# First modulation, second half's norm and its modulation on VectorE alone, GpSimd without arithmetic until the convolution

## Chip, cores and metric

The kernel runs on one core of a Trainium2 chip. The metric is the device time of one execution in microseconds (us). Five engines of the core are named by their roles: TensorE multiplies matrices, VectorE and GpSimd do arithmetic between tiles, ScalarE does activations, scalings and casts, and SyncE (SP) issues the DMA transfers. In the rows of the profile they are PE, DVE, POOL, ACT and SP.

## What is computed

The reference is a stack of two layers on a latent stream x of 1024 tokens by 1024 channels, all in float32. Layer 0 is a convolution module, layer 1 a pooling mixer; each is one modulated sub-layer with a residual:

```python
sh, sc, gt = split(silu(c) @ w_mod[i] + b_mod[i], 3)      # three vectors of 1024
h = rms(x, norm_g[i]) * (1.0 + sc) + sh
x = x + gt * mixer_i(h)

def conv_mixer(h):                                         # layer 0
    a, b, g = split(h @ w_in, 3)
    y = depthwise_conv(a * sigmoid(b), dw, 31 taps) + db
    return (silu(layernorm(y)) * silu(g)) @ w_out

def pool_mixer(h):                                         # layer 1
    v, g = split(h @ w_in, 2)
    pooled = window_mean(v, 2, 4, 8, 16) - v               # one window for each quarter of the channels
    return (group_product(pooled) * scale * silu(g)) @ w_out
```

The context tokens of the full model don't reach the output with two layers.

## The kernel before

The arrays are kept transposed: 128 channels on the partitions, tokens along the free axis. A tile of channels is a "ct" or "kt" (8 of them), and the tokens lie in two halves of 512 (h = 0 and 1). Products run in a split precision: each operand is a high part (ScalarE casts it, `hi_part`) and a low part (VectorE subtracts, `lo_part`), and `mm3` issues three matmuls for a product.

**Layer 0, start.** `load_x(0)` brings the first half of x. `norm_x` squares its tiles on ScalarE and adds them (`squares`, L238 to L250, the add is L248); `rstd_rows` (L217) turns the sum into 1/sqrt on every partition, by small matmuls, a power on GpSimd (L226), a diagonal on VectorE (L208) and a matmul with ones into the one PSUM bank of tag "ax". The modulation vectors are dots of rows of w_mod with silu(c): `dot` (L252) is one instruction on VectorE (L255, `scalar_tensor_tensor` with an accumulator), or a product on GpSimd (L259) and an accumulating copy on ScalarE (L260).

The loop of L354 goes over the 8 blocks of input channels. `mod_block(kt)` loads 512 KB each for the shift and the scale of the block, has the shift's dot done by GpSimd and the scale's by VectorE, and adds the biases (L307, L308). `load_split` loads the first weights of the block, 512 KB, and splits them. `modulate(0, kt)` computes `x*a*r` in one VectorE instruction (L322), the high part (L157) and the low part (L162). Seven PSUM banks (`pf`) collect the products of this block for the first four channel tiles of a and b (FIRST = 4). After block 3 the second half of x is loaded, after block 5 its norm is issued; there GpSimd adds the squares, and the factor is copied from PSUM to SBUF (`rbs[1]`, L375).

Then come the gates of the first half (`gate_ab`, L332: a sigmoid on ScalarE, a product on VectorE, L338), and `modulate(1, kt)` for the second half: a product by the factor on VectorE (even kt) or GpSimd (odd kt) (L326), a scaling on ScalarE (L327), a cast and a subtraction (L156, L161). Next stand 16 dots: eight on GpSimd for gt of layer 0 (`gt0`) and eight on VectorE for sh of layer 1 (`sh1`). The eight for the scale of layer 1 (`a1`) go to a list, `pending`, and are drawn from it by `step(n)`, between the weights of the products that follow.

**Products and convolution.** The first four channel tiles of the second half come next (`pg`), then a loop over ct = 4 to 7 (L455) with the weights wb and wa, each through two rings of four [128, 1024] buffers: "raw" for what is loaded (w_mod too), "w" for the parts. The depthwise convolution (L417) takes a channel tile and a half at a time. Tiles 1, 3, 5 (first half) and 1, 3, 5, 6, 7 (second half) are done by a scaled copy on ScalarE (L435) and an add on GpSimd (L436) for each of 31 taps; the others by VectorE, whose taps (L448) add in two PSUM banks, joined by L453. A tap with a negative offset of the first half needs only y of the first half.

**What sets the order.** Each engine works through a fixed list, which a scheduler writes beforehand from modelled times and priorities; the convolution has the lowest (`priority(LATER * (1 + h))`), so it stands where an engine has nothing else by the model. `behind(...)` puts an engine's instructions after a given one, `ordered` keeps loads in program order. After the products come the gate products (`gate_g`), the layer norm of the first half (`layernorm(0)`: sums on GpSimd and VectorE, L493, a mean, squares), the output product (`out_half`), layer 1 for the first part of the tokens, then the same for the second half. While layer 1 runs, the convolution of the second half is finished, by GpSimd and VectorE, before `layernorm(1)` can start.

Of the kernel before, what the change touches and what calls it, by code (L numbers as in the profile page):

```python
# [12 lines left out]
ALU = mybir.AluOpType  # L13
# [20 lines left out]
DOTS_AHEAD = 2  # L34
# [23 lines left out]
def hybrid_kernel(ctx, tc, xT, vecs, wm, cv_first, cv_w, cv_wo, pl_w, pl_grp, pl_wo, out):  # L58
# [24 lines left out]
    def unit(tag, name, dt=F32, cols=1024):  # L83
        """A [128, 1024] tile in a ring, or in a slot of a region (a letter and a number)."""
        width = WIDTH.get(tag[0], 1024)
        return S.tile([P, width], dt, tag=tag, name=name, bufs=RINGS.get(tag, 1))[:, :cols]
# [43 lines left out]
    # window / count of the positions whose window is cut by an end of the sequence  # L130
# [69 lines left out]
    def gemm(ps, w, r, after=(), start=KT // 2):  # L200
        """The products from start on are issued behind the instructions given."""
        for kt in range(KT):
            with behind(after if kt >= start else ()):
                mm3(ps, cut(w, bl(kt)), r[kt], kt == 0, kt == KT - 1)

    def diagonals(dg, cols):
        """[128, 4, 128] of the four columns, each on the diagonal of a block."""
        return nc.vector.tensor_tensor(  # L208
            out=dg.rearrange("p (j q) -> p j q", j=4),
            in0=ident.unsqueeze(1).broadcast_to((P, 4, P)),  # L210
            in1=cols.unsqueeze(2).broadcast_to((P, 4, P)),
            op=ALU.mult,
        )
# [3 lines left out]
    def rstd_rows(total, name, fill=None):  # L217
        """[128, 512] of 1 / sqrt(sum over the partitions of the total / D + EPS), on every partition."""
        vp = axps(f"vp{name}")
        with priority(-LATER):  # L220
            for j in range(4):
                nc.tensor.matmul(vp[:, j : j + 1], total[:, bl(j)], ones[:, 0:1], start=True, stop=True)
        ve = S.tile([P, 4], F32, tag="ve", name=f"ve{name}", bufs=2)
        scaled = nc.vector.tensor_scalar(ve, vp[:, 0:4], 1.0 / D, EPS, ALU.mult, ALU.add)
        rs = S.tile([P, 4], F32, tag="vr", name=f"vr{name}", bufs=2)
        power_done[0] = nc.gpsimd.tensor_tensor(out=rs, in0=ve, in1=mhalf[:, 0:4], op=ALU.pow)  # L226
        rb = axps(f"rb{name}")
        dg = half("sq", f"dg{name}")
        with priority(-LATER):
            spread = diagonals(dg, rs)  # L230
            done = nc.tensor.matmul(rb, ones, dg, start=True, stop=True)
        if fill is not None:
            fill(GAPS[2], scaled)
            fill(GAPS[3], spread)
        spread_done[0] = spread
        return rb, done

    def squares(xs, name, eng):  # L238
        """A sum of squares over the tiles, which grows by a tile at every call of add."""
# [12 lines left out]
    def dot(w, out, eng):  # L252
        """The sum over the rows of w_mod of their product with silu(c), for 128 of the outputs."""
# [29 lines left out]
    def norm_x(h):  # L283
        total, add = squares(xs[h], f"x{h}", (nc.vector, nc.gpsimd)[h])
# [15 lines left out]
    def mod_block(kt):  # L300
        dots = []
        for part in range(2):
# [3 lines left out]
            dot(w, dots[part], (nc.gpsimd, nc.vector)[part])  # L306
# [8 lines left out]
    def modulate(h, kt):  # L315
# [9 lines left out]
        else:  # L325
            (nc.vector, nc.gpsimd)[kt % 2].tensor_tensor(out=x, in0=x, in1=rbs[1], op=ALU.mult)  # L326
            nc.scalar.activation(x, x, AF.Identity, scale=a, bias=sh)  # L327
            split_to(*hT[h][kt], x)
# [25 lines left out]
    for kt in range(KT):  # L354
# [15 lines left out]
        if kt == 3:  # L370
            load_x(1)
        if kt == 5:
            _, rb = norm_x(1)
            rbs[1] = half("pr", "rbs1")
            nc.scalar.copy(rbs[1], rb)  # L375
# [11 lines left out]
    early = [gemv(0, 2, gt0, nc.gpsimd), gemv(1, 0, sh1, nc.vector)]  # L387
    for i in range(KT):
        with behind(gated if i >= DOTS_AHEAD else []):
            for job in early:  # L390
                next(job, None)
    pending.append(gemv(1, 1, a1, nc.vector))
# [18 lines left out]
    def conv(h, ct, taps=None, count=None):  # L411
        """The convolution of a tile of channels, or the next ones (count) of its taps."""
# [42 lines left out]
    for ct in range(FIRST, KT):  # L455
        wb = load_split(cv_w[KT + ct], f"wb{ct}")
        step(2)
        wa = load_split(cv_w[ct], f"wa{ct}")
        step(2)
# [58 lines left out]
    def gate_norm(h, z, rb):  # L518
        """Normed, gated and split; the norm runs two tiles ahead of the rest."""
# [92 lines left out]
    def load_early(part, k):  # L612
        """One of the weights of the first products of layer 1."""
# [120 lines left out]
    def layer1_out(part, ms, ahead=(), last=None, after=(), start=KT // 2):  # L734
        """The output product: of the first ones (ahead, loaded early) a tile of channels per k, the others in turn."""
# [115 lines left out]
```

## Time and profile before

| What | Value |
|---|---|
| Runs | 811.77, 812.97 and 813.42 us, median 812.97 |
| Profiled execution: span from its first to its last instruction | 810.0 us |
| TensorE busy | 703.4 us (87%) |
| VectorE busy | 671.5 us (83%) |
| GpSimd busy | 566.9 us (70%) |
| ScalarE busy | 407.5 us (50%) |
| DMA | 105.6 MB, mean 130 GB/s |

The profile gives the profiled execution by its span; its own time is not listed apart from that. A busy share is a mean over stages with different limits. A row with a start is an entry of a timeline: start, duration, engine, line of the kernel, operation, what is written and read, and in brackets the idle time ahead of it and what ended that. A row with a count is a group of equal instructions. Names have their buffer numbers left out.

### The profile page before, as it was taken

What the parts mean: (1) busy time and instruction counts of PE and PEld (TensorE: products, weight loads), DVE (VectorE), ACT (ScalarE), POOL (GpSimd) and SP (SyncE); (2) the same over time, 40 slices, a digit from 0 to 9 for tenths busy, and PEclk for the clock granted to TensorE, in tenths of its full rate; (3) what the DMA queues carried; (4) which work ended last, traced back from release to release, by engine and by line L of the source; (5) the groups of instructions that cost most, each with busy time, mean ns of one, the idle gap of its engine ahead of it and who ended that gap; (6) DMA issues with size and microseconds to landing.
All of it is one profiled execution on the core that took longest, in us unless ns stands there. A gap on an engine that the chain in (4) does not pass through costs nothing.

```text
span 810.0 us, 9060 instructions
## 1 busy us (share of the span) xinstructions
PE 703.4 (87%) x3092; PEld 562.2 (69%) x3092; DVE 671.5 (83%) x782; ACT 407.5 (50%) x591; POOL 566.9 (70%) x412
## 2 busy tenths in 40 slices
PE   2887899699999969789899776878799979999998
PEld 1565788488878747468677555656578758888998
DVE  6989999899889799999999899999895572666521
ACT  4543853665666766556766645554332432333210
POOL 3398589999999989789989999898411630444322
PEclk9988999899999989999899978989999989999999
DMA  8673555311012422434521233444642550233232
GB/s 316 239 283 107 189 185 196 104 52 53 27 52 91 168 106 91 144 129 162 179 102 40 78 132 134 137 156 155 233 156 103 158 168 0 91 104 131 79 106 80
DMA packets 36478, 105.63 MB, mean 130 GB/s; under 512 B 4048, under 2 KB 6224, under 8 KB 36432
## 3 DMA queue, kind: packets, MB, share of 16 engines
q1 hardware_dynamic: 36432, 105.05, 37.7%
q8 instruction: 24, 0.39, 0.2%
q14 instruction: 22, 0.18, 0.1%
HBM read 92.45 MB, written 12.58 MB: 130 GB/s over the span
## 4 chain that ended last, share of the span: by engine, by line
DVE 32%; PE 26%; POOL 23%; issue 12%; ACT 4%; DMA 2%; SPq 0%; POOLq 0%; DVEq 0%; ACTq 0%
POOL z L436 18%; DVE cv L448 5%; PE psv L195 2%; PE psv L193 2%; PE psv L194 2%; PE psf L194 2%; PE psf L193 2%; PE psf L195 2%; PE psq L195 2%; PE psq L193 2%; PE psq L194 2%; PE pso L193 2%; PE pso L195 2%; PE pso L194 2%; DVE s L644 2%
## 5 line engine op out<-in xcount | busy, mean ns | idle before, releaser
L436 POOL TENSOR_TENSOR z<-z,pr 128x512 f32<-128x512 f32 (+8 forms) x240 | 381.9, 1592 | 30.7 <-ACT pr L435 16.3
L435 ACT ACTIVATE pr<-y,VT 128x512 f32<-128x512 f32 (+8 forms) x240 | 171.1, 718 | 131.4 <-POOL z L436 128.2
L448 DVE SCALAR_TENSOR_TENSOR cv<-y,VT,cv 128x512 f32<-128x512 f32 (+12 forms) x232 | 160.2, 740 | 0.2
L255 DVE SCALAR_TENSOR_TENSOR wm<-wm,s_row 128x1024 f32<-128x1024 f32 x24 | 44.6, 1861 | 0.1
L640 DVE TENSOR_TENSOR s<-v 128x519 f32<-128x519 f32 (+1 forms) x16 | 21.4, 1341 | 19.5 <-ACT v L689 19.5
L742 DVE SCALAR_TENSOR_TENSOR xf<-psf,gt,xf 128x260 f32<-128x260 f32 (+1 forms) x24 | 13.2, 570 | 29.2 <-PE psf L195 25.2
L259 POOL TENSOR_TENSOR wmb<-wmb,s_row 128x1024 f32<-128x1024 f32 x8 | 22.2, 2772 | 18.2 <-DMA wmb<-in_wm 18.2
L725 DVE SCALAR_TENSOR_TENSOR q<-psy,VT,q 128x260 f32<-128x260 f32 (+1 forms) x24 | 13.5, 569 | 19.2 <-PE psy L195 19.1
L259 POOL TENSOR_TENSOR wm<-wm,s_row 128x1024 f32<-128x1024 f32 x8 | 20.4, 2556 | 12.2 <-DMA wm<-in_wm 12.2
L536 ACT ACTIVATE z<-z,VT 128x512 f32<-128x512 f32 x16 | 12.9, 814 | 27.9 <-DVE z L533 27.9
L644 DVE TENSOR_TENSOR s<-s 128x517 f32<-128x517 f32 (+5 forms) x24 | 22.8, 956 | 0.2
L248 DVE TENSOR_TENSOR vay<-vay,sqy 128x512 f32<-128x512 f32 x14 | 16.5, 1180 | 5.5 <-ACT sqy L247 5.3
L655 DVE SCALAR_TENSOR_TENSOR s<-s,v 128x504 f32<-128x504 f32 (+1 forms) x16 | 19.6, 1235 | 1.4 <-POOL s L653 1.3
L156 ACT CAST y<-q 128x504 fp32r<-128x504 f32 (+1 forms) x16 | 9.9, 616 | 19.7 <-DVE q L725 19.7
L161 DVE TENSOR_TENSOR y<-q,y 128x504 fp32r<-128x504 f32 (+1 forms) x16 | 16.6, 1041 | 3.0 <-ACT y L156 3.0
L161 POOL TENSOR_TENSOR wo16l<-wo,wo16h 128x1024 fp32r<-128x1024 f32 x1 | 2.4, 2393 | 23.5 <-ACT wo16h L156 23.5
L161 DVE TENSOR_TENSOR pd<-s,pd 128x504 fp32r<-128x504 f32 (+1 forms) x16 | 17.5, 1107 | 1.6 <-ACT pd L156 1.4
L255 DVE SCALAR_TENSOR_TENSOR wmb<-wmb,s_row 128x1024 f32<-128x1024 f32 x8 | 15.5, 1933 | 3.0 <-DMA wmb<-in_wm 3.0
L550 DVE SCALAR_TENSOR_TENSOR xr<-pso,gt,xr 128x512 f32<-128x512 f32 x16 | 11.6, 743 | 7.2 <-PE pso L195 7.2
L513 DVE TENSOR_TENSOR va<-va,sqz 128x512 f32<-128x512 f32 x14 | 16.8, 1203 | 0.7
L528 DVE TENSOR_TENSOR z<-z,sgr 128x512 f32<-128x512 f32 x16 | 16.2, 1010 | 1.1 <-ACT z L536 1.1
L156 ACT CAST pd<-s 128x504 fp32r<-128x504 f32 (+1 forms) x16 | 9.7, 617 | 14.5 <-DVE s L655 10.2
(2497 smaller groups left out, 2463.6 us busy)
## 6 DMA issues: line engine op xcount, KB each, us to landing
wm<-in_wm SPq DMA_DIRECT2D x32, 512.0 KB, 3.3
wmb<-in_wm SPq DMA_DIRECT2D x16, 512.0 KB, 6.0
wo<-in_cv_wo SPq DMA_DIRECT2D x16, 512.0 KB, 3.8
wp<-in_pl_wo SPq DMA_DIRECT2D x16, 512.0 KB, 3.2
wg<-in_cv_w SPq DMA_DIRECT2D x12, 512.0 KB, 3.3
wv<-in_pl_w SPq DMA_DIRECT2D x12, 512.0 KB, 3.4
wq<-in_pl_w SPq DMA_DIRECT2D x12, 512.0 KB, 3.3
x<-in_xT SPq DMA_DIRECT2D x16, 256.0 KB, 5.6
```

The costliest lines, as they stand in the source:

```text
L156: return nc.scalar.copy(hi, src)
L161: return eng.tensor_tensor(out=lo, in0=src, in1=hi.bitcast(F32), op=ALU.subtract)
L193: nc.tensor.matmul(ps, w[0], r[0], start=first, stop=False)
L194: nc.tensor.matmul(ps, w[0], r[1], start=False, stop=False)
L195: nc.tensor.matmul(ps, w[1], r[0], start=False, stop=last)
L255: eng.scalar_tensor_tensor(out=w, in0=w, scalar=1.0, in1=s_row, op0=ALU.mult, op1=ALU.mult, accum_out=out)
L259: eng.tensor_tensor(out=w, in0=w, in1=s_row, op=ALU.mult)
L435: nc.scalar.activation(pr[:, o], y[:, i], AF.Copy, scale=dw(k))
L436: nc.gpsimd.tensor_tensor(out=z[:, o], in0=z[:, o], in1=pr[:, o], op=ALU.add)
L448: nc.vector.scalar_tensor_tensor(out=a[:, o], in0=y[:, i], scalar=dw(k), in1=a[:, o], op0=ALU.mult, op1=ALU.add)
L640: nc.vector.tensor_tensor(out=s[:, :m], in0=v[:, :m], in1=v[:, 1 : m + 1], op=ALU.add)
L644: nc.vector.tensor_tensor(out=s[:, :m], in0=s[:, :m], in1=s[:, step : step + m], op=ALU.add)
```

## The change

The eight shift dots of the first modulation go from GpSimd to VectorE. The sum of squares of the second half goes from GpSimd to VectorE; its x is loaded after block 5 instead of block 3, its norm is issued behind the whole loop, and its factor is read from PSUM instead of an SBUF copy. The second half's modulation gets the form of the first: one VectorE instruction for `x*a*r`, a high part with the shift on ScalarE, a low part with the shift on VectorE. The dots of gt0 and sh1 leave their place behind that modulation; all 24 dots are now on VectorE and in `pending`, and are drawn three at a time between the weights of ct = 5, 6 and 7 (none at ct = 4), with the rest at the `step(100)` behind the loads of the output weights. Docstrings and comments change too.

```diff
 def norm_x(h):
-        total, add = squares(xs[h], f"x{h}", (nc.vector, nc.gpsimd)[h])
+        total, add = squares(xs[h], f"x{h}", nc.vector)
...
-            dot(w, dots[part], (nc.gpsimd, nc.vector)[part])
+            dot(w, dots[part], nc.vector)
...
         else:
-            (nc.vector, nc.gpsimd)[kt % 2].tensor_tensor(out=x, in0=x, in1=rbs[1], op=ALU.mult)
-            nc.scalar.activation(x, x, AF.Identity, scale=a, bias=sh)
-            split_to(*hT[h][kt], x)
+            nc.vector.scalar_tensor_tensor(out=x, in0=x, scalar=a, in1=rbs[1], op0=ALU.mult, op1=ALU.mult)
+            hi_part(hT[h][kt][0], x, sh)
+            lo_part(*hT[h][kt], x, sh)
...
-        if kt == 3:
+        if kt == 5:
             load_x(1)
-        if kt == 5:
-            _, rb = norm_x(1)
-            rbs[1] = half("pr", "rbs1")
-            nc.scalar.copy(rbs[1], rb)
+    _, rbs[1] = norm_x(1)
...
-    early = [gemv(0, 2, gt0, nc.gpsimd), gemv(1, 0, sh1, nc.vector)]
-    for i in range(KT):
-        with behind(gated if i >= DOTS_AHEAD else []):
-            for job in early:
-                next(job, None)
-    pending.append(gemv(1, 1, a1, nc.vector))
+    pending += [gemv(0, 2, gt0, nc.vector), gemv(1, 0, sh1, nc.vector), gemv(1, 1, a1, nc.vector)]
...
         wb = load_split(cv_w[KT + ct], f"wb{ct}")
-        step(2)
+        step(3 if ct > FIRST else 0)
         wa = load_split(cv_w[ct], f"wa{ct}")
-        step(2)
+        step(3 if ct > FIRST else 0)
```

## Rows read from the trace of the kernel before

**Rows 1.** Busy time of each engine in two stretches: us, instructions, TensorE clock, DMA share, GB/s.
```profile
40.00:60.00 20.00, 16.14 (x64) 12.74 (x62) 16.32 (x15) 9.59 (x14) 19.74 (x9) 0.83 0.76 283
118.50:560.00 441.50, 382.88 (x1560) 299.89 (x1558) 421.27 (x487) 271.67 (x391) 405.01 (x281) 0.94 0.32 112
```

**Rows 2.** The page: a line of the chain (part 4) and two groups (part 5).
```profile
POOL z L436 18%; DVE cv L448 5%; PE psv L195 2%; PE psv L193 2%; PE psv L194 2%; PE psf L194 2%; PE psf L193 2%; PE psf L195 2%; PE psq L195 2%; PE psq L193 2%; PE psq L194 2%; PE pso L193 2%; PE pso L195 2%; PE pso L194 2%; DVE s L644 2%
L436 POOL TENSOR_TENSOR z<-z,pr 128x512 f32<-128x512 f32 (+8 forms) x240 | 381.9, 1592 | 30.7 <-ACT pr L435 16.3
...
L255 DVE SCALAR_TENSOR_TENSOR wm<-wm,s_row 128x1024 f32<-128x1024 f32 x24 | 44.6, 1861 | 0.1
```

**Rows 3.** Timelines of VectorE and GpSimd, 555 to 564 us: start us, us, instruction.
```profile
555.41 0.68 DVE L453 TENSOR_TENSOR z<-z,cv 128x512 f32<-128x512 f32 x1
...
561.49 2.87 DVE L493 TENSOR_TENSOR zsum<-zsum,z 128x512 f32<-128x512 f32 x1
...
557.63 1.71 POOL L436 TENSOR_TENSOR z<-z,pr 128x497 f32<-128x497 f32 x1
```

**Rows 4.** Groups of GpSimd, 0 to 118.5 us: count, busy us, mean ns, idle before and releaser.
```profile
L259 POOL TENSOR_TENSOR wmb<-wmb,s_row 128x1024 f32<-128x1024 f32 x8 | 22.2, 2772 | 18.2 <-DMA wmb<-in_wm 18.2
...
L259 POOL TENSOR_TENSOR wm<-wm,s_row 128x1024 f32<-128x1024 f32 x8 | 20.4, 2556 | 12.2 <-DMA wm<-in_wm 12.2
...
L248 POOL TENSOR_TENSOR vax<-vax,sqx 128x512 f32<-128x512 f32 x7 | 12.0, 1709 | 6.0 <-ACT sqx L247 5.7
...
L326 POOL TENSOR_TENSOR x<-x,rbs 128x512 f32<-128x512 f32 x4 | 7.4, 1871 | 0.5 <-ACT rbs L375 0.5
```

**Rows 5.** VectorE's timeline, 0 to 92 us.
```profile
13.43 2.46 DVE L255 SCALAR_TENSOR_TENSOR wmb<-wmb,s_row 128x1024 f32<-128x1024 f32 x1 [0.82 <-DMA wmb<-in_wm]
...
16.13 0.15 DVE L307 TENSOR_TENSOR sh<-dot,VT 128x1 f32<-128x1 f32 x1
17.21 2.83 DVE L208 TENSOR_TENSOR dgx<-ident,vrx 128x512 f32<-128x512 f32 x1 [0.93 <-POOL vrx L226]
...
21.09 3.36 DVE L255 SCALAR_TENSOR_TENSOR wmb<-wmb,s_row 128x1024 f32<-128x1024 f32 x1
...
27.62 1.22 DVE L255 SCALAR_TENSOR_TENSOR wmb<-wmb,s_row 128x1024 f32<-128x1024 f32 x1
...
30.75 2.24 DVE L307 TENSOR_TENSOR sh<-dot,VT 128x1 f32<-128x1 f32 x1
...
82.89 0.74 DVE L162 SCALAR_TENSOR_TENSOR h06l<-x,sh,h06h 128x512 fp32r<-128x512 f32 x1
...
90.49 2.68 DVE L161 TENSOR_TENSOR h14l<-x,h14h 128x512 fp32r<-128x512 f32 x1
```

**Rows 6.** Groups of VectorE, 0 to 92 us.
```profile
L248 DVE TENSOR_TENSOR vax<-vax,sqx 128x512 f32<-128x512 f32 x7 | 4.8, 692 | 2.8 <-ACT sqx L247 2.1
...
L322 DVE SCALAR_TENSOR_TENSOR x<-x,a,rbx 128x512 f32<-128x512 f32 x1 | 0.7, 740 | 0.0
```

**Rows 7.** GpSimd's timeline, 92 to 118.5 us.
```profile
92.58 3.95 POOL L436 TENSOR_TENSOR z<-z,pr 128x511 f32<-128x511 f32 x2
...
98.86 2.40 POOL L259 TENSOR_TENSOR wm<-wm,s_row 128x1024 f32<-128x1024 f32 x1 [2.32 <-DMA wm<-in_wm]
...
116.13 2.40 POOL L259 TENSOR_TENSOR wm<-wm,s_row 128x1024 f32<-128x1024 f32 x1 [2.38 <-DMA wm<-in_wm]
```

**Rows 8.** Groups of VectorE, 518 to 553 us.
```profile
L255 DVE SCALAR_TENSOR_TENSOR wm<-wm,s_row 128x1024 f32<-128x1024 f32 x3 | 5.6, 1878 | 0.0
...
L161 DVE TENSOR_TENSOR y<-q,y 128x504 fp32r<-128x504 f32 x1 | 2.9, 2896 | 0.0
```

**Rows 9.** Two waits by engine (us in total, times, longest), and VectorE's timeline.
```profile
ACT h06h L157 <- DVE sh L307: 12.5, 2, 7.5
...
PE ps L193 <- ACT wa4h L156: 7.9, 1, 7.9
...
281.56 2.11 DVE L161 TENSOR_TENSOR wg40l<-wg,wg40h 128x1024 fp32r<-128x1024 f32 x1 [4.26 <-ACT wg40h L156]
```

More of the change, by code (lines that the diff above doesn't have):

```diff
@@ L33 @@
 H1_AHEAD = 4
-DOTS_AHEAD = 2
 ZORD = ((0, 1, 2, 3, 4, 6, 5, 7), (0, 1, 2, 3, 5, 6, 7, 4))
```

## The prediction

> **What bounds the kernel now.** I read the busy time by stretch first, then the chain that ended last, then the timelines of the two engines it names. Between 118.5 and 560 us VectorE is busy 421 of 441.5 us and GpSimd 405 [rows 1]; TensorE is not full there. The chain names GpSimd's convolution adds (L436) with 18% of the span, more than three times the next line, VectorE's convolution taps (L448) [rows 2]. Both finish together: the last add starts at 557.6 us, the last convolution step of VectorE (L453) at 555.4, and only then do the sums of the second norm (L493) close [rows 3]. Behind 560 us VectorE has room. So the change is worth what it moves these two ends, and the later of them counts; I take VectorE's for that.
>
> **Removed: VectorE's stalls.** In the first 92 us GpSimd runs 8 dots of 2.77 us, 7 adds of 1.71 and 4 products of 1.87; 8 more dots of 2.56 lie up to 118.5 [rows 4]. Beside each, an instruction of VectorE with two inputs in SBUF stretches. A dot (L255) takes 1.22 us alone and 3.36 beside a GpSimd dot; a [128, 1] add (L307) takes 0.15 and 2.24 [rows 5]. In the VectorE timeline from the dot at 13.43 us (2.46) to the subtraction at 90.49 (2.68), 21 instructions stand above the shortest of their shape; their excess sums to 31 us. With no GpSimd arithmetic there but the two small powers (L226, which stay), I take all 31 as gone: **-31**. Some 6.6 us more lie beside the last four GpSimd dots, behind 92 us; there the convolution takes GpSimd's place, so I take 0 for them and keep -6.6 as an end.
>
> **Added to VectorE.** Eight dots of the first modulation at 1.22 each [rows 5], 9.8 us. Seven adds of the second norm at 0.69 (first half's, alone) [rows 6], 4.8. In the second half's modulation eight products of three operands at 0.74 [rows 6] replace four of two at 0.68 [rows 3], and the low part gets a third operand too, 0.06 longer: 5.9 - 2.7 + 0.5, some 3.7 us. These products read their factor from a PSUM bank; the one instruction of L322 that does so took those 0.74 us. Together **+18.3**. The eight dots of gt0 follow later, beside the convolution, so at the mean of all such dots, 1.86 [rows 2]: **+14.9** (at 1.22 it would be 9.8). ScalarE loses the accumulating copies of 16 dots and eight scalings (L327); it has 170 of 441.5 us free [rows 1], so I count nothing, though its casts stand in one queue behind waits on GpSimd, and if that cover fails, VectorE's waits return.
>
> **GpSimd's end.** Its first add starts at 92.58 us, behind a gate (L338) that needs the first half's products [rows 7]. The first block is modulated 5.5 us earlier: 2.15 us of the diagonal's stretch and the 3.36 us dot that began at 21.09, right ahead of it, go [rows 5]; its product then starts near 19.2. From there a block costs VectorE two dots and a weight's low part of the same 1024 columns at 1.22, the product and the low part of the block at 0.74 each, and the two [128, 1] steps, 0.4: some 5.6 us; with 1.5 for the first block's parts, the seven others end near 60 us, against 83.6 now (the low part h06l) [rows 5]. The x load of the second half, eight transfers of 256 KB, moves in the SP queue from ahead of blocks 4 and 5 to ahead of blocks 6 and 7. 2.1 MB at 283 GB/s [rows 1] are 7.4 us, in which VectorE may stand. Between 60 and 67 I take 63.6, so 20 us earlier. The four GpSimd dots among the first adds (9.6 us) and GpSimd's two waits for their loads (4.7) go too [rows 7]: the adds end some **34 us earlier**, if y arrives in time. It should: 15 taps of channel tiles 1 and 3 need only the first half, 30 adds or 48 us of cover at 1.59 each.
>
> **The tail.** VectorE thus has its last 34 us without GpSimd. From 518 to 553 us its stretched instructions, from the three dots (1.88 for 1.22) to the subtraction of 2.90 us for 0.68, 17 in all, hold 13.4 us above the shortest of their shape [rows 8]. 13.4 / 35 x 34 is **-13.0**. The last sum of L493, 2.87 us beside GpSimd, takes 0.68: **-2.2**.
>
> **Queues.** Today 16 w_mod loads stand in SP's queue ahead of the weights of channel tile 4, and TensorE waits 7.9 us for the cast of the second of these, which stands on ScalarE behind copies paced by GpSimd [rows 9]. Afterwards no dot is stepped beside tile 4, and 18 of 24 go by threes beside tiles 5 to 7, in the ring of four buffers that the weights use; six are left for the step before the norm. I count nothing for TensorE: its 7.9 us and some 15 us of an earlier start lie off VectorE's end. If VectorE had room they would count.
>
> **The sum.** -31 + 18.3 + 14.9 - 13.0 - 2.2 = **-13.0 us** on the profile's 810.0 us, so 797.0. The median of the runs is 3.0 us above that span; kept as it is, 800.0. A measurement of this kernel can tell about 0.2%, 1.6 us, from no change.
>
> **The rivals.**
> *All ends move (0.25).* VectorE has 20 us of holes between 118.5 and 560 [rows 1], as the 4.3 us before wg40 [rows 9], where a ScalarE cast is late. With GpSimd ahead and ScalarE lighter, up to 14 of these close: -27, 786. For it: such casts stand behind copies that wait for GpSimd's adds, as tile 4's did. Against: the order is fixed beforehand, and the casts may be placed as late.
>
> *VectorE is late for the first norm (0.12).* All its work until the mean of the first half (283 us) grows by 18.3 + 14.9 - 31 = 2.2 us, and the wedge of the x load adds up to 7.4: +9.6, so 822.6, if the end hangs on that norm and what follows it, not on the sum of VectorE's work. It decides once VectorE stands idle after 300 us for want of data. Against: VectorE hardly stands between 300 and 557 us, and the second norm waits on the filling taps.
>
> *It doesn't come to pass (0.08).* The convolution is low-priority work placed by a modelled clock; GpSimd may just stand idle where its dots were and begin its adds near 92 us. Then -31 + 18.3 + 14.9 is all: 815 at worst; with 2 to 4 us of shorter waits about 813, no change.
>
> *Work on a full engine is paid in full (0.03).* If the stalls were an artefact of how records are written and not lost time, VectorE would gain 33.2 us of work and lose none: 846. ScalarE's waits for those [128, 1] adds, 12.5 us in two [rows 9], speak against it. The Trainium skill (Perfetto Trace Analysis, Optimizing Scalar/DVE Operations) has the rule behind this rival: where VectorE is saturated, move work away, perhaps even to GpSimd; it adds that the two share a read port, so that this might not help. The trace bears out the second half more than the first.
>
> **How the numbers follow.** The forecast has 0.52 (its own range 792 to 809: 10 us up for the x load and the gt0 dots, 8 down for the 6.6 and the shorter gt0 dots), the rivals 0.25, 0.12, 0.08 and 0.03. Faster is the first two, 0.77; the same 0.08; slower 0.15. The range leaves out the two slower rivals and the lowest part of the first: 784 to 812.
>
> **What would show it.** Right: no GpSimd arithmetic but two powers before the convolution; L255 on wmb near 1.22 and L307 near 0.15; the first add of L436 near 73 us and without gaps; the last near 524; VectorE's last L453 about 11 us earlier, near 545. Wrong: the dots at 1.9 again in the first 60 us (another stall), a wait of VectorE for wmb or x of over 8 us, TensorE standing for weights of tiles 5 to 7 behind dots in the ring, or the mean of the first norm later than 283 us.

## The result, and the profile after

The changed kernel takes **804.68 us** (median of 4 runs, 802.07 to 805.21) against 813.05 us for the kernel before (4 runs beside it, 811.77 to 813.42): ratio 0.9885, 95% interval 0.9865 to 0.9906. It is faster by 8.4 us; 13.0 were forecast. The profiled span went from 810.0 to 802.4 us.

In the changed file the helpers have line numbers lower by one: the dot is L254 (was L255), the split L160 (L161). From the convolution on they are lower by nine: GpSimd's add L427 (L436), VectorE's last convolution step L444 (L453), the last sum L484 (L493).

First the groups of VectorE from 0 to 92 us in the changed kernel, the counterpart of [rows 6]:

```profile
L254 DVE SCALAR_TENSOR_TENSOR wmb<-wmb,s_row 128x1024 f32<-128x1024 f32 x16 | 19.3, 1216 | 0.0
L247 DVE TENSOR_TENSOR vax<-vax,sqx 128x512 f32<-128x512 f32 x14 | 9.6, 686 | 2.5 <-ACT sqx L246 2.2
...
L325 DVE SCALAR_TENSOR_TENSOR x<-x,a,rbx 128x512 f32<-128x512 f32 x8 | 5.4, 742 | 0.2 <-PE rbx L230 0.2
L321 DVE SCALAR_TENSOR_TENSOR x<-x,a,rbs 128x512 f32<-128x512 f32 x7 | 5.2, 743 | 0.0
```

All sixteen dots of the first modulation now run at 1.216 us, the shortest seen in [rows 5]; the fourteen adds at 0.686 and the products at 0.74 are undisturbed too. Now VectorE's timeline and GpSimd's around the gate:

```profile
30.71 0.15 DVE L306 TENSOR_TENSOR sh<-dot,VT 128x1 f32<-128x1 f32 x1
...
60.02 0.75 DVE L161 SCALAR_TENSOR_TENSOR h06l<-x,sh,h06h 128x512 fp32r<-128x512 f32 x1
```
```profile
59.03 1.94 POOL L225 TENSOR_TENSOR vrx<-vex,mhalf 128x4 f32<-128x4 f32 x1 [43.06 <-DVE vex L223]
79.08 21.52 POOL L427 TENSOR_TENSOR z<-z,pr 128x511 f32<-128x511 f32 x14 [18.12 <-ACT z L423]
```

The add of one column that took 2.24 us takes 0.15. The first half is modulated at 60.8 us instead of 83.6 [rows 5], and GpSimd's adds start at 79.08 us instead of 92.58 [rows 7], fourteen in a row without a gap.

To see where the time went I cut both executions at four instructions of VectorE: the first gate product (y out of pf), the first subtraction of the mean in the first norm, the first normed product of the first half, and that of the second half. I call the stretch up to the first of these the front, and the time that VectorE stands idle in a stretch its holes. The windows view, before and after (columns as in [rows 1]: length, then busy time of TensorE, its weight loads, VectorE, ScalarE, GpSimd, each with its count; TensorE clock, DMA share, GB/s):

```profile
0.00:89.30 89.30, 59.51 (x196) 42.78 (x197) 76.00 (x85) 45.10 (x71) 54.09 (x59) 0.90 0.65 230
89.30:283.59 194.29, 183.43 (x782) 147.69 (x781) 178.94 (x239) 117.29 (x173) 179.57 (x116) 0.98 0.32 109
283.59:314.93 31.34, 23.35 (x91) 17.93 (x90) 30.46 (x32) 19.59 (x29) 26.43 (x18) 0.84 0.28 101
314.93:588.95 274.02, 226.79 (x901) 173.58 (x900) 265.78 (x279) 158.60 (x230) 237.55 (x165) 0.93 0.39 135
588.95:810.00 221.05, 210.33 (x1129) 180.19 (x1128) 120.33 (x152) 66.87 (x89) 69.23 (x56) 0.98 0.32 107
```
```profile
0.00:65.63 65.63, 49.57 (x187) 37.06 (x188) 56.94 (x103) 28.37 (x40) 4.86 (x37) 1.00 0.86 314
65.63:268.06 202.43, 190.24 (x796) 151.36 (x795) 192.38 (x256) 117.22 (x169) 178.32 (x117) 0.97 0.29 96
268.06:307.56 39.50, 21.77 (x78) 16.03 (x77) 38.55 (x42) 21.27 (x32) 33.53 (x21) 0.77 0.43 138
307.56:580.56 273.00, 229.89 (x908) 176.83 (x908) 257.95 (x277) 152.20 (x221) 227.47 (x156) 0.93 0.41 134
580.56:802.40 221.84, 213.00 (x1129) 182.43 (x1128) 121.31 (x152) 66.79 (x89) 69.79 (x56) 0.97 0.33 106
```

Read the length and VectorE's busy time (third pair). The front is 23.7 us shorter. The next two stages take 16.3 us of that back: VectorE has five of the eight dots of gt0 there, and six dots of the second modulation's scale that had not fitted in the products, at 1.7 to 2.3 us each between 257.9 and 280.5 us; the first norm's stage grows by 8.2 us. What is left at the first normed product is 7.4 us. The long stage from there to the second norm's product gains one more microsecond, though VectorE has 7.8 us less to do in it, and the last stage gains nothing.

In one sum: up to the second norm's product VectorE is busy 551.2 us before and 545.8 after, and its holes are 37.8 and 34.7 us. That is **-5.4 of work and -3.0 of holes**, 588.95 to 580.56.

The tail, where the forecast was off: GpSimd's timeline from its last add on, then VectorE's, both of the changed kernel.

```profile
520.66 6.82 POOL L427 TENSOR_TENSOR z<-z,pr 128x500 f32<-128x500 f32 x4
527.56 2.16 POOL L484 TENSOR_TENSOR zsum<-zsum,z 128x512 f32<-128x512 f32 x1
529.67 2.38 POOL L160 TENSOR_TENSOR wp40l<-wp,wp40h 128x1024 fp32r<-128x1024 f32 x1
533.12 2.34 POOL L160 TENSOR_TENSOR wo10l<-wo,wo10h 128x1024 fp32r<-128x1024 f32 x1 [1.07 <-ACT wo10h L155]
538.34 2.38 POOL L160 TENSOR_TENSOR wo11l<-wo,wo11h 128x1024 fp32r<-128x1024 f32 x1 [2.88 <-ACT wo11h L155]
540.69 2.83 POOL L160 TENSOR_TENSOR wp50l<-wp,wp50h 128x1024 fp32r<-128x1024 f32 x1
543.48 2.83 POOL L160 TENSOR_TENSOR wo12l<-wo,wo12h 128x1024 fp32r<-128x1024 f32 x1
546.27 2.83 POOL L160 TENSOR_TENSOR wo13l<-wo,wo13h 128x1024 fp32r<-128x1024 f32 x1
```
```profile
530.31 2.82 DVE L160 TENSOR_TENSOR wp30l<-wp,wp30h 128x1024 fp32r<-128x1024 f32 x1
...
533.70 2.31 DVE L635 TENSOR_TENSOR s<-s 128x517 f32<-128x517 f32 x1
...
539.14 4.94 DVE L635 TENSOR_TENSOR s<-s 128x513 f32<-128x513 f32 x2
543.99 2.86 DVE L160 TENSOR_TENSOR y<-q,y 128x504 fp32r<-128x504 f32 x1
546.77 0.73 DVE L439 SCALAR_TENSOR_TENSOR cv<-y,VT,cv 128x497 f32<-128x497 f32 x1
547.41 2.23 DVE L160 TENSOR_TENSOR y<-q,y 128x504 fp32r<-128x504 f32 x1
...
550.21 1.27 DVE L635 TENSOR_TENSOR s<-s 128x505 f32<-128x505 f32 x2
551.40 0.68 DVE L444 TENSOR_TENSOR z<-z,cv 128x512 f32<-128x512 f32 x1
552.18 0.69 DVE L484 TENSOR_TENSOR zsum<-zsum,z 128x512 f32<-128x512 f32 x1
```

The adds did end 32 us earlier, at 527.5 instead of 559.3. But GpSimd isn't idle behind them: it goes straight on to the low parts of output weights (wp40 and wp50, and wo10 to wo13; the kernel before split these last four from 561 us on), and beside each of them an instruction of VectorE is as long as it was beside an add. Six instructions (the two of 4.94 are one row) stand 10.7 us above the shortest of their shape: 1.6 + 1.6 + 3.7 + 2.2 + 1.6. VectorE ends 4.0 us earlier instead of 11.

### The profile page after: what moved, and what is told of

Read it like the earlier page. It is cut to its first block, busy times and chain, and to the rows that moved or that the text cites. A ratio compares the mean times of both kernels' runs of the same rounds, so it can differ in the third digit from the quotient of the medians.

```text
span 802.4 us, 9019 instructions
## 1 busy us (share of the span) xinstructions
PE 704.5 (88%) x3092; PEld 563.7 (70%) x3092; DVE 667.1 (83%) x825; ACT 385.9 (48%) x550; POOL 514.0 (64%) x385
## 4 chain that ended last, share of the span: by engine, by line
POOL 32%; PE 30%; DVE 19%; issue 12%; ACT 6%; DMA 1%; SPq 0%; POOLq 0%; DVEq 0%; ACTq 0%
POOL z L427 28%; PE psf L192 2%; PE pso L194 2%; PE psf L193 2%; PE psf L194 2%; PE pso L193 2%; PE pso L192 2%; DVE wmb L254 2%; PE psv L194 2%; PE psq L194 2%; PE psv L193 2%; PE psv L192 2%; PE psq L193 2%; PE psq L192 2%; ACT pr L426 2%
## 5 line engine op out<-in xcount | busy, mean ns | idle before, releaser
L427 POOL TENSOR_TENSOR z<-z,pr 128x512 f32<-128x512 f32 (+8 forms) x240 | 387.9, 1617 | 47.9 <-ACT z L423 18.1
L254 DVE SCALAR_TENSOR_TENSOR wm<-wm,s_row 128x1024 f32<-128x1024 f32 x32 | 54.6, 1707 | 3.6 <-DMA wm<-in_wm 3.4
L225 POOL TENSOR_TENSOR vrx<-vex,mhalf 128x4 f32<-128x4 f32 x2 | 3.0, 1484 | 55.5 <-DVE vex L223 43.1
L716 DVE SCALAR_TENSOR_TENSOR q<-psy,VT,q 128x260 f32<-128x260 f32 (+1 forms) x24 | 13.6, 569 | 19.3 <-PE psy L194 19.1
L635 DVE TENSOR_TENSOR s<-s 128x517 f32<-128x517 f32 (+5 forms) x24 | 25.9, 1085 | 0.2
L160 DVE TENSOR_TENSOR y<-q,y 128x504 fp32r<-128x504 f32 (+1 forms) x16 | 17.9, 1125 | 3.0 <-ACT y L155 3.0
L254 DVE SCALAR_TENSOR_TENSOR wmb<-wmb,s_row 128x1024 f32<-128x1024 f32 x16 | 19.3, 1216 | 0.0
L160 DVE TENSOR_TENSOR pd<-s,pd 128x504 fp32r<-128x504 f32 (+1 forms) x16 | 15.3, 971 | 3.3 <-ACT pd L155 3.1
L541 DVE SCALAR_TENSOR_TENSOR xr<-pso,gt,xr 128x512 f32<-128x512 f32 x16 | 11.7, 743 | 7.5 <-PE pso L194 7.5
L160 POOL TENSOR_TENSOR wo16l<-wo,wo16h 128x1024 fp32r<-128x1024 f32 x1 | 2.7, 2671 | 23.5 <-ACT wo16h L155 23.5
L646 DVE SCALAR_TENSOR_TENSOR s<-s,v 128x504 f32<-128x504 f32 (+1 forms) x16 | 16.3, 1030 | 1.5 <-POOL s L644 1.3
L192 PE MATMUL psy<-pd,grs 128*128 128x260 f32 (+1 forms) x48 | 14.9, 323 | 3.1 <-ACT pd L155 2.1
L155 ACT CAST pd<-s 128x504 fp32r<-128x504 f32 (+1 forms) x16 | 9.7, 615 | 15.8 <-DVE s L646 11.5
L225 POOL TENSOR_TENSOR vrz<-vez,mhalf 128x4 f32<-128x4 f32 x2 | 2.0, 1017 | 23.6 <-DVE vez L223 23.6
L194 PE MATMUL psy<-pd,grs 128*128 128x260 f32 (+1 forms) x48 | 15.2, 319 | 0.0
```

What stands on the lines that cost most here:

```text
L155: return nc.scalar.copy(hi, src)
L160: return eng.tensor_tensor(out=lo, in0=src, in1=hi.bitcast(F32), op=ALU.subtract)
L192: nc.tensor.matmul(ps, w[0], r[0], start=first, stop=False)
L194: nc.tensor.matmul(ps, w[1], r[0], start=False, stop=last)
L254: eng.scalar_tensor_tensor(out=w, in0=w, scalar=1.0, in1=s_row, op0=ALU.mult, op1=ALU.mult, accum_out=out)
L427: nc.gpsimd.tensor_tensor(out=z[:, o], in0=z[:, o], in1=pr[:, o], op=ALU.add)
```

## The experiments

In what follows "first norm" and "second norm" are the times of the first normed product of each half (307.56 and 580.56 us in the changed kernel). One caution for all of them: where the front is untouched, its end still differs by 2 to 3 us between profiled executions (65.6 us in the profile above, at a mean granted TensorE clock of 1.00 there; 67.5 to 68.3 in e1, e2, e3, e9 and e10, at 0.85 to 0.95). These runs were made on three chips; what makes the difference is not shown. So some 2 of the 23.7 us of the front may belong to that one execution, and a mark that differs by less than 3 us says little by itself.

**1. The stall of the first dots, undone (e4).** The eight shift dots of the first modulation go back to GpSimd; all else is as changed.

```
-            dot(w, dots[part], nc.vector)
+            dot(w, dots[part], (nc.gpsimd, nc.vector)[part])
```


> The changed kernel with one part undone: the eight shift dots of the first modulation on GpSimd and ScalarE again. In the changed kernel a dot of this stage takes VectorE 1.22 us, in the one before 1.93. If GpSimd's products stall VectorE, the first stage (to the first gate, 64 us) gets longer although VectorE loses eight dots of 1.2 us: the other eight go to 1.7 us or more, the low parts stretch, and the stage ends 5 to 12 us later; the end 3 to 8 us later, near 809 to 812. If a full VectorE simply pays for what is put on it, taking eight dots away shortens the stage by up to 10 us.

Measured: 812.82 us (811.23 to 815.5), ratio 1.0009 (0.9996 to 1.0021): 8.1 us behind the changed kernel, as slow as before. The front ends at 81.1 us, 15.4 later, where 5 to 12 had been expected. The remaining eight dots of VectorE:

```profile
L254 DVE SCALAR_TENSOR_TENSOR wmb<-wmb,s_row 128x1024 f32<-128x1024 f32 x8 | 15.6, 1946 | 0.6 <-DMA wmb<-in_wm 0.6
L247 DVE TENSOR_TENSOR vax<-vax,sqx 128x512 f32<-128x512 f32 x14 | 13.7, 975 | 3.6 <-ACT sqx L246 2.4
```

Eight dots cost 15.6 us here, sixteen cost 19.3 in the changed kernel. VectorE has ten instructions fewer in the front and is busy 70.0 us instead of 56.9. ScalarE has eight accumulating copies back too, so this run alone doesn't separate the stall from them.

**2. The stall by itself (e7).** Sixteen extra GpSimd products of [128, 512], two behind each block of the first half, into a buffer that nothing reads. VectorE's work is that of the changed kernel.

```
         modulate(0, kt)
+        for i in range(2):
+            part = hT[0][kt][0].bitcast(F32)
+            nc.gpsimd.tensor_tensor(out=half("sg", f"scrap{kt}{i}")[:, :HW], in0=part, in1=part, op=ALU.mult)
```


> The changed kernel with sixteen more GpSimd products of [128, 512] behind the blocks' modulation, two a block, on data that nobody waits for; VectorE's list of work is unchanged. If a GpSimd product with two inputs in SBUF stalls a VectorE instruction with two inputs in SBUF, VectorE's instructions of the first stage stretch by 0.7 to 1.1 us per product: its busy time in the first 75 us grows by 11 to 17 us and the first gate comes as much later; the end 5 to 12 us later. If the long records of before were an artefact of the records, or caused by something else, the stage keeps its length.

Measured: 816.93 us (815.98 to 819.01), ratio 1.0055 (1.0041 to 1.0069), 12.2 us behind the changed kernel. The windows view, first two stages:

```profile
0.00:77.17 77.17, 51.51 (x182) 37.44 (x183) 69.44 (x102) 27.44 (x39) 28.21 (x53) 0.87 0.73 263
77.17:280.22 203.05, 191.88 (x799) 151.93 (x799) 193.57 (x256) 117.88 (x170) 178.86 (x117) 0.97 0.29 97
```

GpSimd has 23.4 us more to do in the front, and VectorE's busy time there grows by 12.5 us (56.94 to 69.44) with 102 instructions for 103. The front ends 11.5 us later, and all of it reaches the end: second norm 592.8, 12.2 later. This is the cleanest evidence for the main theory: VectorE was given no work, ScalarE none, and the kernel lost what VectorE's instructions were stretched by.

**3. The second half on GpSimd again (e5).** The sum of squares, four of the eight products, the form of the modulation and the early load of x are as in the kernel before.

```
-        total, add = squares(xs[h], f"x{h}", nc.vector)
+        total, add = squares(xs[h], f"x{h}", (nc.vector, nc.gpsimd)[h])
...
-            nc.vector.scalar_tensor_tensor(out=x, in0=x, scalar=a, in1=rbs[1], op0=ALU.mult, op1=ALU.mult)
+            (nc.vector, nc.gpsimd)[kt % 2].tensor_tensor(out=x, in0=x, in1=rbs[1], op=ALU.mult)
...
```


> The changed kernel with another part undone: the second half's x loaded after block 3, its sum of squares on GpSimd, its modulation in the form of before (four of eight products on GpSimd, a scaling on ScalarE, a cast, a subtraction). Stall theory: the first stage grows by the stalls beside 7 adds and 4 products, 3 to 8 us, the end by as much less what the holes ahead of the first norm take up: 806 to 811. Paid-in-full theory: VectorE loses 8 us of work, the end comes earlier, 797 to 802.

Measured: 818.54 us (812.31 to 820.59), ratio 1.0068 (1.0049 to 1.0087): 13.9 us lost, more than expected. The front, and VectorE's busy time in it (third pair), grow by 11.7 and 11.9 us:

```profile
0.00:77.37 77.37, 53.35 (x184) 37.80 (x185) 68.80 (x104) 33.21 (x49) 25.55 (x48) 0.93 0.74 267
```

Up to the second norm VectorE's busy time is 546.1 us, no more than the 545.8 of the changed kernel, though this part took work off it that the prediction priced at 8.5 us (4.8 and 3.7): the stretch has filled what the work left. On top of that its holes are 47.8 us instead of 34.7. VectorE waits 8.5 us for ScalarE's casts of wb6 and wb7 (1.0 for that of wb6 in the changed kernel) and 5.0 instead of 3.4 for loads of dots. So this part is paid by the stretch that I had costed and by holes that I had not; why just these casts come late was not followed further.

**4. The first part alone (e12).** The kernel before with its sixteen dots on VectorE, nothing else.

```
-            dot(w, dots[part], (nc.gpsimd, nc.vector)[part])
+            dot(w, dots[part], nc.vector)
```


> The kernel before with one edit: the 8 shift dots of the first modulation on VectorE, all else as before. Theory (a GpSimd product stalls VectorE beside it): the 16 dots of the first modulation take 1.2 to 1.4 us each instead of 1.9 for 8, the 8 of GpSimd (22 us) are gone, VectorE's own work rises by 8 x 1.22 = 9.8 less the sums of halves: the front ends 3 to 8 us earlier, 805 to 810 in all. Rival (the front ends when the late x tiles and the rest of GpSimd's work let it): 811 to 814. Rival (VectorE pays for the dots in full): 820 to 823.

Measured: 810.67 us (807.12 to 813.89) beside 813.61 for before, ratio 0.9971 (0.995 to 0.9992). The time lies between what the theory and its first rival had said. The sixteen dots take 1.41 us each, for GpSimd still has its adds and products in the front. The gate comes 7.4 us earlier (81.95), the first norm 3.1 (311.79), the second not at all (589.29); in this profiled execution, one of the kernel's fastest (807.63 us), the gain lies in the last stage, 216.4 us for 221.1 at a granted clock of 0.99 for 0.98. Undone from the changed kernel this part is worth 8 us, alone 3: the parts don't add up, and a front that ends earlier is not by itself a kernel that ends earlier.

**5. Where the later dots stand.** Five variants move the 24 dots of gt0, sh1 and a1. e1 takes four a step (at both places), so that all are done before the first norm, e9 three a step from channel tile 4 on, and e2 asks for the rest behind the first norm.

```
-        step(3 if ct > FIRST else 0)
+        step(4 if ct > FIRST else 0)
```


> The changed kernel, with four instead of three dots drawn at each place beside channel tiles 5 to 7, so that all 24 are done before the first norm. Two theories. A (the prediction's: the sum of VectorE's work sets the end): the six dots only change places, so the time stays within 2 us of the changed kernel's 804.7. B (the end of the first norm sets it, and a chain of 268 us that does not depend on GpSimd's or VectorE's load follows): the stretch from the first subtraction of the mean to the first product by 1/sqrt shrinks from 39.5 us to about 31, the 31.3 of the kernel before, and the end comes 5 to 8 us earlier, 797 to 800, less what the dots cost VectorE ahead of the mean.

> The changed kernel with three dot steps in every product from the first on, instead of none in the first product of that stage: the 24 dots are all done before the first norm, and begin 8 to 10 us after the gate. Theory (dots only change places on a VectorE that is full): 803 to 808, as with four a step. Rival (the six dots inside the first norm cost their full time, so that having none there gains): first normed product 5 to 8 us earlier, 797 to 800.

```
-    step(100)
     early_taps = conv_taps(1, 0)
...
     y1, done = gate_norm(0, z, rb)
+    step(100)
```


> The changed kernel with its last six dots drawn behind the first half's gated norm instead of ahead of the norm. A (the sum of VectorE's work sets the end): no change, 803 to 806. B (the end of the first norm sets it): the norm's 39.5 us shrink to about 31 and the mean itself comes no later, perhaps 3 us earlier since three of the dots stand ahead of it: 794 to 798.

Measured: e1 807.48 us (805.23 to 809.9; ratio 0.991 to 0.9945), e9 805.84 (803.9 to 807.63; 0.9888 to 0.9938), e2 810.24 (807.91 to 810.95; 0.9939 to 0.9969). In e1 and e9 no dot is left in the first norm, whose stage is 35.9 and 35.7 us instead of 39.5; the stage ahead of it is longer by 4.2 and 1.9. The six late dots gained nothing by standing elsewhere in the products: e9 can't be told from the change, and e1 is some 3 us slower, which neither of its two theories had. e2 did not do what it was for: the order planned beforehand put its dots back between 269 and 304 us, where VectorE stood 4.9 us for a load. It tells nothing of dots behind the norm.

e6 gives gt0 back to GpSimd, places gt0 and sh1 early as the kernel before does, and steps two at a time; e11 is e6 with gt0 on VectorE.

```
-    pending += [gemv(0, 2, gt0, nc.vector), gemv(1, 0, sh1, nc.vector), gemv(1, 1, a1, nc.vector)]
+    early = [gemv(0, 2, gt0, nc.gpsimd), gemv(1, 0, sh1, nc.vector)]
+    for i in range(KT):
+        with behind(gates[-1] if i >= 2 else []):
+            for job in early:
+                next(job, None)
+    pending.append(gemv(1, 1, a1, nc.vector))
...
-        step(3 if ct > FIRST else 0)
+        step(2)
```


> The changed kernel with the third part undone: gt0 on GpSimd and sh1 on VectorE right behind the second half's modulation, the rest by twos from tile 4 on, as before. By the account of VectorE's time, its work until the first norm falls by the eight gt0 dots (15 us) less the stalls of GpSimd's eight products (12 us), while GpSimd's adds start some 20 us of work later and end near 545 instead of 527; tile 4's weights come behind 16 loads again. If only VectorE's time counts: 801 to 805, no change. If GpSimd's start counts for the end: 808 to 812.

> The changed kernel with the dots of gt0 and sh1 placed early and two a step as before, but with those of gt0 kept on VectorE; it differs from the 800.7 us kernel by the engine of 8 dots alone. Theory (the dots of gt0 cost VectorE their time wherever they stand, 8 x 1.2 to 1.9 = 10 to 15 us before the first norm, against 2.4 us each on GpSimd where they end in time): first normed product 5 to 9 us later than with gt0 on GpSimd, 804 to 809 in all. Rival (it was the late placing in the products that cost, not the engine): 799 to 802.

Measured: e6 **800.74 us** (799.58 to 801.98), ratio 0.9852 (0.984 to 0.9865); e11 804.07 (799.03 to 806.94), ratio 0.9888 (0.9857 to 0.9919). e6 is the fastest of all; against before its interval touches that of the change at 0.9865, and the two did not run on one chip. The windows view of e6, then of e11, the two stages from the first norm's mean on:

```profile
268.01:299.84 31.83, 26.15 (x105) 19.66 (x104) 30.95 (x32) 20.25 (x30) 27.37 (x19) 0.89 0.31 106
299.84:576.27 276.43, 228.23 (x899) 173.71 (x898) 270.92 (x279) 159.31 (x230) 238.63 (x165) 0.92 0.41 134
```
```profile
264.57:301.82 37.25, 30.01 (x116) 22.49 (x115) 33.85 (x34) 23.64 (x35) 32.62 (x22) 0.86 0.30 106
301.82:579.61 277.79, 229.09 (x901) 174.42 (x900) 269.92 (x279) 155.96 (x226) 233.70 (x161) 0.92 0.39 134
```

In e6 the gate comes 10 us later than in the changed kernel (75.9), and GpSimd's adds end 19 us later (546.5), near the 545 expected; the kernel is faster all the same. The first norm comes 7.7 (e6) and 5.7 us (e11) earlier, the second 4.3 and 1.0. Both do more work on VectorE up to there (549.2 and 551.7 us against 545.8) and have fewer holes (27.1 and 27.9 against 34.7). Between the norms the changed kernel's VectorE waits 3.2 us for a gate product of TensorE, and TensorE had stood 6.0 us ahead of that, inside the first norm's stage, for the low part of wg60; in e6 the first of these waits is absent and the second 3.9. The two placings have the fewest holes of all runs, but two dots a step are not the whole reason: the kernel before and e12 draw two a step as well and have 37.8 and 37.5. The engine of gt0 makes 2.0 us at the first norm and 3.3 at the second, less than the 5 to 9 I had expected at the first: eight dots on GpSimd free VectorE of their time but stretch what runs beside them. The profiled execution of e11 is its fastest run, with a last stage of 217.6 us; its median stands with the changed kernel. By times alone e6 and e11 are hardly apart.

One thing holds here that I had not looked for. In all fourteen kernels of this document but e3 and e10 (below) the stretch between the two normed products takes 273.0 to 277.8 us, while VectorE is busy 257.9 to 270.9 us in it: where it has less to do there, it mostly stands longer. What sets that length is open. The sum of VectorE's work doesn't set it alone, and neither does the first norm with a fixed chain behind it (theory B of e1): in e6 and e11 less than the 7.7 and 5.7 us arrive at the second norm, in e12 nothing of its 3.1.

**6. The start of GpSimd's adds (e8).** ScalarE writes the first term of GpSimd's convolution into a buffer that holds the second half's x tiles 2 and 3; in the changed kernel it waits 4.4 us there for the low part of h12 (the waits view names L161), so the adds start at 79.08 and not at 73. e8 modulates these two tiles ahead of 0 and 1.

```
-    for kt in range(KT):
+    for kt in (2, 3, 0, 1, 4, 5, 6, 7):
         with behind(gates[0][:1] if kt >= H1_AHEAD else []):
             modulate(1, kt)
```


> The changed kernel with the second half's channel tiles 2 and 3 modulated ahead of 0 and 1. They lie in the buffer that the convolution result of tiles 1 and 3 takes over, and GpSimd's first add waits for that. If this buffer gates GpSimd's start, the first add comes 2 to 4 us earlier than 79.1 us; if the gate of the first products does, it stays. The end: unchanged by B; by a theory that GpSimd's adds set the end, 2 to 4 us earlier.

Measured: 809.57 us (808.26 to 812.94), ratio 0.9966 (0.9943 to 0.9989), slower than the change. The adds start at 80.65 us: 1.4 to 1.9 earlier than the 82.0 to 82.5 of e1 to e3 on the same chip, which is less than a mark can tell, and not the 2 to 4 ahead of 79.1 that were expected. They end at 533.4, later than any of these three. So e8 doesn't settle what an earlier start would be worth; e6, whose adds start at 84.65 and which is the fastest, shows that it is not needed.

**7. The tail (e3, e10).** e3 holds the four early splits of the second output weights behind the power of the second norm; e10 behind a one-column copy of VectorE's last sum. (In both, wp40 and wp50 stay ahead of the norm.)

```
-    with behind([sums_done[1]]):
+    with behind([power_done[0]]):
         ws = [load_split(cv_wo[m], f"wo1{m}", ("Q", 2 * m), eng=nc.gpsimd) for m in range(4)]
```


> The changed kernel with GpSimd's four splits of the second output weights held behind the power of the second norm, so that VectorE's last work before that norm runs without GpSimd. The forecast's tail term was 13 us: by it VectorE's last convolution step ends some 8 us earlier than 551 us, and the end moves by as much less what the late weights cost the output product (four splits of 2.4 us, up to 10 us). By B (a chain of data from the first norm on) VectorE's instructions get shorter but its work is not what ends last: the last step moves by under 3 us and the end by 0, or later by the weights' delay.

```
-        zsum = half("vs", f"zsum{h}")
+        zsums[h] = zsum = half("vs", f"zsum{h}")
...
-    with behind([sums_done[1]]):
+    summed = const.tile([P, 1], F32, name="summed")
+    copied = nc.gpsimd.tensor_copy(summed, zsums[1][:, :1])
+    with behind([copied]):
         ws = [load_split(cv_wo[m], f"wo1{m}", ("Q", 2 * m), eng=nc.gpsimd) for m in range(4)]
```


> The changed kernel, with the four early splits of the second output weights on GpSimd held behind a one-column copy of VectorE's last sum, so that none of them runs beside VectorE's last convolution (in the changed kernel they run from 533.1 to 549.1 us, VectorE's last convolution ends at 551.4 + about 0.7). Theory (those splits are what ate the forecast gain of the tail): VectorE's last join about 4 to 6 us earlier against the first normed product than in the changed kernel, the splits start within 2 us of the last sum, first to second normed product 266 to 268 us instead of 273, and the stage behind it stays at 221 to 223 because the weights come about 20 us earlier than when they were held behind the power: 798 to 801. Rival (the four weights are needed by then in any case, as when they were held behind the power): the last stage grows to 225 to 227, total 802 to 805. Second rival (the tail is not set by the splits): the join does not move, 804 to 806.

Measured: e3 803.44 us (802.55 to 806.56; ratio 0.9874, 0.9858 to 0.989), e10 803.08 (800.48 to 804.95; 0.9881, 0.9855 to 0.9907): neither can be told from the change, and for e10 798 to 801 had been expected. VectorE's timeline in e10, over the end of the convolution and into the second norm:

```profile
542.10 0.67 DVE L160 TENSOR_TENSOR y<-q,y 128x504 fp32r<-128x504 f32 x1
...
547.34 0.67 DVE L444 TENSOR_TENSOR z<-z,cv 128x512 f32<-128x512 f32 x1
...
553.93 1.29 DVE L496 TENSOR_TENSOR z<-z,mu 128x512 f32<-128x512 f32 x2 [2.92 <-PE mu L490]
...
556.00 2.54 DVE L505 TENSOR_TENSOR va<-va,sqz 128x512 f32<-128x512 f32 x1
558.46 2.82 DVE L160 TENSOR_TENSOR y<-q,y 128x504 fp32r<-128x504 f32 x1
```

From the first norm to L444 it is 236.5 us (310.80 to 547.34) against 243.8 in the changed kernel, so the splits did cost 7.3 us there: the theory of the tail is right as far as that (4 to 6 had been expected). Then the splits run from 550.4 to 560.7 us beside the norm, whose instructions are stretched in turn (4.0 us in the last two rows above), and VectorE stands 2.9 us for TensorE's mean. Of the 7.3 us, 1.4 are left at the second norm (271.65 us of stage against 273.00). In e3 the norm is undisturbed too, as the last two stages show (this execution is e3's longest, 806.56 us):

```profile
310.98:577.46 266.48, 226.78 (x908) 174.83 (x908) 250.96 (x278) 151.41 (x220) 220.06 (x154) 0.94 0.39 129
577.46:804.80 227.34, 215.13 (x1129) 183.31 (x1128) 125.20 (x152) 67.81 (x90) 77.17 (x59) 0.96 0.34 113
```

VectorE is busy 251.0 us between the norms, 14.8 less than in the kernel before: with the splits gone, nearly the whole 15.2 us that the forecast had for the tail come off VectorE's work. The stage is 266.5 us. But the splits then lie behind 572 us, beside the normed products, and the last stage takes 227.3 us for 221.8, with TensorE waiting 3.0 us for the split parts of the second half's output. The work must run somewhere, and in neither place was it free.

## Why the prediction was right, and where not

The direction and the mechanism of the stall were right. That the size came out as near as it did is in part luck, for the gain lies elsewhere than forecast: the sum had +2.2 us ahead of the first norm and -15.2 behind it; measured are -7.4 at the first normed product and -1.0 between the two.

*Removed and added work: right.* -31 + 18.3 + 14.9 = +2.2 us of VectorE's work up to the first norm was forecast; busy time there went from 285.4 to 287.9, **+2.5**. The rows named as signs came out: dots at 1.216, the [128, 1] add at 0.15, no GpSimd arithmetic but two powers before the convolution. That the two sums agree so closely is luck too: the eight dots of gt0 took 11.2 us and not 14.9 (three stand ahead of the gate, at 1.2), so the other terms were some 4 us dearer together; which, was not followed. e7 shows that the mechanism is the stall and not an artefact of records, and e4 agrees: with GpSimd work put back, real time is lost, 12 and 8 us. The last rival (846 us) falls with them. The Trainium skill (Perfetto Trace Analysis, Optimizing Scalar/DVE Operations) says that moving work from a saturated VectorE, perhaps to GpSimd, may make sense, and warns that the two share a read port, so that it might not help. In the front the warning holds here: e4's eight dots on GpSimd lost 8.1 us. Later it doesn't show: with gt0's eight dots on GpSimd (e6) the kernel takes 800.74 us, with them on VectorE (e11) 804.07.

*The x load: too dear.* Half of a wedge of 7.4 us was taken. The first half was modulated at 60.8 us, at the lower end of 60 to 67; no wedge shows.

*GpSimd's end: near.* First add 79.08 for 73; 4.4 of these 6 us are ScalarE's wait for the buffer that I had not looked up. The last add ended at 527.5 for 524.

*The tail: wrong, by the term and by what it was to set.* "VectorE thus has its last 34 us without GpSimd" is the step that failed. It gave -13.0, and -2.2 for the last sum. The last sum came as said (0.69 us). But GpSimd took the splits of the output weights forward into the 34 us, and the stretch went on: in place of -15.2 the work between the norms fell by **7.8 us**. e10 measures what the four splits cost in that place, 7.3 us, nearly the whole difference. What I missed was to ask what the freed engine does next. The second step that failed is "the later of them counts; I take VectorE's": of the 7.8 us that did come, 1.0 shortened the stage, and in e3 7.5 of 14.8 did. The rest became holes.

*Holes: counted at nothing, -3.0 in the end.* Ahead of the first norm's product 10 us of them closed (29.5 to 19.7; 4.6 of these in the front, the rest behind it, as the rival "all ends move" had it), and between the norms 6.8 opened (8.2 to 15.1), by no rival. "Late for the first norm" did not come: its mean was subtracted 15.5 us earlier. "It doesn't come to pass" did not either: the adds moved forward.

So -5.4 of work, -3.0 of holes and +0.8 in the last stage make -7.6 in the span, where -13.0 was forecast; the medians differ by 8.4. (The forecast's own range should have ended at 810: 800 and 10.) What stays open: what sets the length between the two norms, and why the change's placing of dots leaves 7 us more holes than that of e6 and e11.

## What to carry to other kernels

Where VectorE is the bound, cost a GpSimd instruction by the stretch of what VectorE runs beside it as well as by its own time: here 23.4 us of GpSimd products cost 12.2 us of the kernel without adding anything to VectorE. It is a price for a stretch in which VectorE has few holes; e6 gave eight dots back to GpSimd and was not slower for it. When an engine is freed, look in its list for the next piece of work that may move forward, and ask what that runs beside, before counting the freed stretch as gain. And when less work doesn't give a shorter time, read the engine's holes beside its busy time: between the norms VectorE had 20 us less to do in e3 than in e6, and the stage was 10 us shorter.

## What the runs showed of the hardware

Not every VectorE instruction is stretched beside GpSimd. The convolution taps, which read one operand from SBUF and accumulate in a PSUM bank, are not: 232 of them in the changed kernel, most beside a GpSimd that is busy 83 to 88% of the stages in which they stand. The view by line of the changed kernel (count, then shortest, median and longest in ns, first and last start in us, shapes):

```profile
L439 DVE SCALAR_TENSOR_TENSOR cv<-y,VT,cv x232: 725/741/756, 85.0 to 549.6; 128x512 f32<-128x512 f32 x60, 128x501 f32<-128x501 f32 x6, 128x503 f32<-128x503 f32 x6, 128x505 f32<-128x505 f32 x6
...
L635 DVE TENSOR_TENSOR s<-s x24: 676/712/2874, 445.7 to 745.6; 128x517 f32<-128x517 f32 x6, 128x533 f32<-128x533 f32 x6, 128x513 f32<-128x513 f32 x4, 128x529 f32<-128x529 f32 x4
```

No tap took over 0.756 us; the window sums of L635, both inputs in SBUF and of about the same size, go from 0.676 to 2.874. So with its accumulators in PSUM VectorE's convolution runs beside GpSimd's without being stretched; no run here has them in SBUF, so what that would cost is not measured.
